# Modulation products of a two-layer hybrid block: column groups of the array and the shape of a loaded piece

## The chip, the core and the metric

One core of a Trainium2 chip. Metric: device time of one execution in microseconds (us). The kernel before takes 3295.98 us, the median of three runs (3289.71 to 3297.98). Engines are called as the profile calls them: PE (matmul), PEld (the weight load that goes with each matmul), DVE, ACT, POOL, and SP, whose queue SPq issues all DMAs here.

## The reference

Two layers (`DEPTH = 2`) over 1024 latent and 256 context tokens of 1024 features. Each layer begins with the modulation vectors, which the change is about; everything else uses them:

```
mod = silu(c) @ w_ada + b_ada            # w_ada: 1024 x 6144 per layer
sh1, sc1, g1, sh2, sc2, g2 = split(mod, 6)
cmod = silu(c_ctx) @ w_ada + b_ada       # the same weights for the context tokens
p = (x * (1 + sc1) + sh1) @ w_in         # then attention, convolution, mLSTM, w_out
x = layer_norm(ALPHA * x + g1 * y)
x = layer_norm(ALPHA * x + g2 * mlp(x * (1 + sc2) + sh2))
```

So per layer a vector of 1024 features is multiplied by a 1024 x 6144 matrix in float32, for two vectors (c and c_ctx). The matrix has 25 MB per layer and is read once.

## The kernel before, in words

The kernel is a program of one core in which a tile framework puts in the waits. Float32 accuracy of the large products comes from splitting both sides into a rounded part and a rest and summing three products in the PE's reduced float32 form. The modulation products are plain float32; the profile shows each of those matmuls as two records, that is two passes of the PE, each with a weight load.

**The modulation products (`ada_steps`, L160).** The 6144 columns of a layer are three rounds of 2048. A round has four 512-column chunks j = 0 to 3. The two vectors stand in `self.sil[:, k]`, 128 features by 32 columns (two used, the rest zero); they are the stationary side. The output of chunk j goes to the partitions 32j to 32j + 31 of one PSUM bank, so that it is made by the j-th group of 32 columns of the array. A round's sum runs over eight feature blocks k. The work is cut into closures, one for each loaded piece `wada`: a closure does the products of its piece and then issues the load of a later piece (`load(i + ahead)`, L187). A piece has n columns, n = 1024 / div:

- For the first layer, rounds 1 and 2 (L2027): div 1, pieces of 128 x 1024 (512 KB), four buffers, four loads ahead. The closures are taken by `tick(2)` in `p1_mlstm`, two after each token tile of the key and value projections (names `mk_ps`, `mv_ps`, lines L77 to L79). Round 0 of this layer has its own function, `ada_first`, which the change leaves alone.
- For the second layer, all three rounds: div 2, pieces of 128 x 512 (256 KB), two buffers, one load ahead. Round 0 (L2128) is done within the first layer's `mlp1`, one closure after every fourth step of its column loop (names `c_ps`, `cx_ps`). Rounds 1 and 2 (L2142) are done within the first layer's `mlp2`, one closure after every third product (names `o_ps`). All of these large products are issued at line L1365.

When a round's sum is complete, `fin` (L190) adds the bias on DVE, transposes four blocks on the PE (`adat`) and writes the vectors.

**What sets the order.** Each engine takes its instructions in the order in which the program was built, apart from a few that the framework moves. All loads and stores go through the one queue SPq in order; the load of a piece waits for the closure that last used its buffer. In `mlp2` the loads of hidden tiles (`hb`, L1643) and of weights (`rw`, L1347) stand in the same queue and wait for their own buffers.

**What mlp1 and mlp2 do.** Both are products in Winograd's form of 2 x 2 blocks. In `mlp2`, for every product of six (or three) matmuls of 512 columns, DVE or ACT adds or copies the result bank `o_ps` into `acc`, while DVE, ACT and POOL make the split operands `xs_hi`, `xs_lo` and `wm` of later products. In the second layer's `mlp2` there are no modulation products.

Of the kernel before, what the change touches and what calls it, by code (L numbers as in the profile page):

```python
# [14 lines left out]
PSUM = bass.MemoryType.PSUM  # L15
# [18 lines left out]
# columns of the regrouped input projection: a0 g0 | a1 g1 | mq | mk | mv mg | mo | cq ckv kr  # L34
COL_CONV, COL_MQ, COL_MK, COL_MV, COL_MO, COL_CQ = 0, 512, 768, 1024, 1296, 1552

# per-partition constants of a layer
# [8 lines left out]
class Kern:  # L46
# [11 lines left out]
    # ---------------------------------------------------------------- helpers  # L58
# [4 lines left out]
    def after(self, ins, prev):  # L63
        """issue ins behind prev (same engine)"""
        self.tc.add_manual_dep(ins.ins, prev.ins.name, mybir.DependencyInfo(
            mybir.DependencyClass.NoSync, mybir.DependencyReason.DATA), reason="pace")
        return ins

    def release_held(self, prev, n=1):
        """the n oldest sets of transposes kept back are issued behind prev"""  # L70
        for _ in range(min(n, len(self.held))):
            for ins in self.held.pop(0):
                self.after(ins, prev)
# [20 lines left out]
    def rsqrt_steps(self, pool, out, x, scale, eps, n):  # L94
        """out = 1 / sqrt(x * scale + eps) on [p, n], from an integer estimate and Newton steps; an instruction a step."""
# [15 lines left out]
    def rsqrt_act_steps(self, pool, out, x, scale, eps, n=1):  # L111
        """The same from ScalarE's square root and a Newton step."""
# [18 lines left out]
    # ---------------------------------------------------------------- set-up  # L131
# [28 lines left out]
    def ada_steps(self, l, rounds, raw_pool, ps, sm_pool, bufs, sm_tag="ada_bs", tag="wada", ahead=None, div=1):  # L160
        """Modulation vectors, four 512-column chunks a round: 0 sh1 sc1, 1 g1 sh2, 2 sc2 g2. A list of closures,
        each the products of one loaded piece and the load of a later one."""
# [6 lines left out]
        def load(i):  # L169
            if i < len(items):  # L170
                r, k, c0 = items[i]
                raw[i] = raw_pool.tile([P, n], F32, name="wada", tag=tag, bufs=bufs)
                nc.sync.dma_start(raw[i], a["w_ada"][l, r, k, :, c0:c0 + n])

        def step(i):
# [6 lines left out]
            w = raw.pop(i)  # L182
            for jj in range(n // 512):
                j = c0 // 512 + jj
                nc.tensor.matmul(acc[r][32 * j:32 * j + 32], self.sil[:, k], w[:, jj * 512:(jj + 1) * 512],  # L185
                                 start=(k == 0), stop=(k == KT - 1))
# [24 lines left out]
    def ada_first(self, raw_pool, ps, sm_pool, bufs):  # L211
        """sh1 and sc1 of the first layer by halves of the features. A closure a half."""
# [3 lines left out]
        def half(h):  # L216
# [4 lines left out]
            # even k in the rows 0:64, odd k in the rows 64:128  # L221
# [20 lines left out]
    # ---------------------------------------------------------------- split streams: hi / lo tiles [128, tile, k, 128 tokens]  # L242
# [14 lines left out]
    def make_u0(self, u, tmp, kk):  # L257
        """The modulated stream of the first layer, four feature blocks."""
# [9 lines left out]
    # ---------------------------------------------------------------- input projection  # L268
    def load_w(self, pool, src, c0, n, tag="w"):
        """columns c0:c0+n of a [128, 8, N] weight as split tiles of four k each."""  # L270
# [25 lines left out]
    # ---------------------------------------------------------------- phase 1: everything read from the modulated stream  # L296
    def p1_mlstm(self, l, u, last, ps, wp, hk, ml, steps, w=None):
        """mLSTM query (feature-major), key, value and gates (token-major)."""
# [12 lines left out]
        # the first layer's stream comes by halves of its features  # L311
# [36 lines left out]
    def residual_steps(self, l, pool):  # L348
        """Closures: alpha * (normalised stream * ln2_g + ln2_b) of the layer before, a token tile each, in place."""
# [16 lines left out]
    def residual_consts(self, l, pool, tag, bufs):  # L366
        """Constant part of the second residual, alpha * ln1_b + g2 * b_mlp2, of both kinds of tokens to DRAM."""
# [10 lines left out]
    def p1_conv(self, l, u, last, ps, wp, tmp):  # L378
        """Gated linear unit of the conv group (twice its value; the halves are in the taps)."""
# [17 lines left out]
    def p1_mla(self, l, u, last, ps, wp, wx, raw):  # L397
        """Compressed q / kv and the rotary key of a token tile, with the mean squares of their rms norms."""
# [25 lines left out]
    # ---------------------------------------------------------------- conv: depthwise taps, layer norm over channels, swish  # L424
    def conv_steps(self, l, last, ps, acc, tp, pool):
        """Closures in order: taps of channel half 0 on VectorE, half 1 on GpSimd, then the norm and swish."""
# [7 lines left out]
        def tap(t, dve, pool_):  # L434
            # behind the given instructions of the two engines
# [61 lines left out]
    def spill(self, pool, c, t0, src):  # L497
        """256 tokens of a row block of the concatenated heads, split and kept in DRAM until the output projection."""
# [6 lines left out]
    # ---------------------------------------------------------------- bidirectional mLSTM  # L505
    def mlstm_gates(self, ps, gp, sm):
        """Stabilised gate quantities. Row r = dir * 64 + tile * 4 + head, tokens along the free axis."""
# [70 lines left out]
        # decay of every chunk on the partitions of its head  # L578
# [15 lines left out]
    def mlstm(self, l, last, ps, ml, wk):  # L594
        nc = self.nc
        nto = NLT if last else NT
        # chunk states: every chunk's own update goes to its successor's slot, then the recurrence runs in place
# [72 lines left out]
    def mlstm_out(self, l, u, last, pm, wp, S, wk):  # L670
        """Output gate from its own projection, per-head normalisation of a pair of token tiles; its rows of the
        concatenated heads."""
# [18 lines left out]
        def pair(t0):  # L691
# [6 lines left out]
            # statistics of the eight (tile, head) rows; H holds twice the gated value  # L698
# [12 lines left out]
    # ---------------------------------------------------------------- latent attention  # L711
    def mla_norm(self, l, last, gi, tmp):
        """Normalised compressed q / kv of a group of tokens, in place."""
# [11 lines left out]
    def mla_rotate(self, tmp):  # L725
        """Rotary shared key, in place."""
# [13 lines left out]
    def mla_prep(self, l, last, ps, A, tmp, gi):  # L740
        """Compressed q / kv and the shared key of a group of tokens, feature-major, the former split."""
# [28 lines left out]
    def mla_values(self, l, ps, wq, A):  # L770
        """Values of all heads, token-major."""
# [20 lines left out]
    def attention(self, l, last, psc, ps, X, wq, A1, A, B, wqk0, taps, post):  # L792
        """Software pipeline over units of (head, 128 queries): scores of unit i are issued between the transposes of
        unit i - 2, the value products of an earlier group and the projections of a later one. The units of the
        context queries (256 of a head in one) lie between those of the last latent group of their head pair."""
        nc, a = self.nc, self.a
        sc = psc.tile([P, 2560], F32, name="sc")
        # buffers in the place of the stream: transposed exponentials; split keys and queries
# [116 lines left out]
        def transpose_parts(i, E, kts):  # L915
# [11 lines left out]
            while i0 < nk:  # L927
                # runs of consecutive key tiles, four to a bank
# [90 lines left out]
    # ---------------------------------------------------------------- rows, norms  # L1019
# [5 lines left out]
    def row_stats(self, pool, r, sm, tagp, junk, jb=2):  # L1025
        """(-mean, 1/std, -mean/std) of a token tile [128, 1024]; its row sums are in sm, else VectorE alone takes them."""
# [15 lines left out]
    def row_stats_steps(self, pool, st, r, sm, junk, jb, root=False):  # L1042
        """The same from row sums, the instructions behind the squares one by one."""
# [12 lines left out]
    def norm_rows(self, pool, r, sm, tagp, junk, jb=2):  # L1056
        """r = (r - mean) * rstd over the 1024 columns of a token tile."""
        st = self.row_stats(pool, r, sm, tagp, junk, jb)
        return self.nc.scalar.activation(r, r, AF.Identity, scale=st[:, 1:2], bias=st[:, 2:3])

    def next_stream(self, ps, x, t0, nt, rows, sc, sh, tmp, tag, hold=False):
        """rows: normalised token tiles t0..t0+nt; writes x = split(rows^T * sc + sh)."""
# [13 lines left out]
    def affine_cols(self, l, g0, b0, sc, sh, name):  # L1076
        """per-feature scale and shift of a modulated layer-normed stream: g*sc1, b*sc1 + sh  ([128, k, 2])"""
# [9 lines left out]
    # ---------------------------------------------------------------- output projection, first layer norm  # L1087
# [3 lines left out]
    def to_mats(self, ps, rows, sc, sh, pool, hold=False):  # L1091
        """rows: an even and an odd normalised token tile. For each kk the blocks B of rows^T * sc + sh (feature blocks
        kk, kk + 4 by the two tiles) and the sums T of them, split, in the order B11 T3 B21 B22 | T1 T2 T4. The four stages."""
# [35 lines left out]
    def xblock(self, xs, bx, c, s, kk, i):  # L1129
        """operand i of feature blocks kk, kk + 4 for the token pairs 2c, 2c + 1 (s: high or low part)"""  # L1130
# [8 lines left out]
    def xdst(self, xs, bx, pr):  # L1139
        """where to_mats puts its results for a pair of token tiles"""  # L1140
# [19 lines left out]
    def out_proj(self, l, last, p1, pw, ps, xs, W1, W2, R, R2):  # L1160
# [4 lines left out]
        def slot(s, t):  # L1165
            # the first four in the place of the first matrices, then a ring of three
# [9 lines left out]
        # weights, split, resident: the first three row blocks in W1; concatenated heads  # L1176
# [24 lines left out]
        def finish(t):  # L1201
            """residual, first norm, residual of the second norm"""
# [4 lines left out]
            while len(kept) > (t == 4 and not last) and t != 9:  # L1207
                # stores behind the loads that the next products wait for
# [32 lines left out]
            if t >= NLT:  # L1241
                # kept in memory until the space for its operands is free
# [10 lines left out]
        def gate(t, hf):  # L1253
            """the residual is in the row's place"""
# [14 lines left out]
        # the first tiles run side by side while weights arrive; the last ones are done early with the weights of W1  # L1269
# [37 lines left out]
        # the stages of the last two tiles' norms  # L1307
# [25 lines left out]
    def rslots(self, n):  # L1333
        """rows of two hidden tiles: three pairs of places in turn, those of the second product behind those of the first"""
# [19 lines left out]
    # ---------------------------------------------------------------- MLP, second layer norm  # L1354
# [917 lines left out]
```

## Time and profile before

| what | value |
|---|---|
| median of three runs | 3295.98 us (3289.71 to 3297.98) |
| profiled execution: span from first to last instruction | 3292.5 us |
| instructions | 49295 |
| DMA | 337.17 MB, mean 102 GB/s |

The page gives the span of the profiled execution; it does not tell a separate time with what lies around it. The span is 3.5 us under the median and within the three runs.

How to read the rows: a row of the timeline has its start, the time until its last instruction's end, engine, line, operation, names (out<-in), shape and count; equal instructions that follow each other are merged. Ends of matmuls are modelled, and rows overlap, so the pace of the PE is read from the starts of successive rows. A bracket tells idle time before a row and what ended it. `128*32 128x512` is an array of 128 rows by 32 columns with 512 columns streamed.

### The profile page before, as it was taken

What the parts mean: (1) busy time and instruction counts of PE and PEld (TensorE: products, weight loads), DVE (VectorE), ACT (ScalarE), POOL (GpSimd) and SP (SyncE); (2) the same over time, 40 slices, a digit from 0 to 9 for tenths busy, and PEclk for the clock granted to TensorE, in tenths of its full rate; (3) what the DMA queues carried; (4) which work ended last, traced back from release to release, by engine and by line L of the source; (5) the groups of instructions that cost most, each with busy time, mean ns of one, the idle gap of its engine ahead of it and who ended that gap; (6) DMA issues with size and microseconds to landing.
All of it is one profiled execution on the core that took longest, in us unless ns stands there. A gap on an engine that the chain in (4) does not pass through costs nothing.

```text
span 3292.5 us, 49295 instructions
## 1 busy us (share of the span) xinstructions
PE 3124.8 (95%) x18778; PEld 2540.8 (77%) x18778; DVE 2153.8 (65%) x3914; ACT 1356.8 (41%) x2572; POOL 1322.3 (40%) x1138
## 2 busy tenths in 40 slices
PE   7999999999899999999998999999999899999986
PEld 4778877777789999766677777877767799977775
DVE  3275688755854433767779445588757855578997
ACT  2122566672433333432332621466663433343332
POOL 0021488320221111466665251266411422258885
PEclk9999999999899999999999998999999899999998
DMA  8521100026433233444334332100025333333322
GB/s 263 187 68 40 49 18 17 14 83 225 159 120 101 97 99 103 157 126 144 114 109 134 142 111 50 56 21 14 14 92 213 109 109 108 106 128 97 102 94 105
DMA packets 179021, 337.17 MB, mean 102 GB/s; under 512 B 14016, under 2 KB 85696, under 8 KB 178784
## 3 DMA queue, kind: packets, MB, share of 16 engines
q1 hardware_dynamic: 178784, 334.03, 31.6%
q8 instruction: 147, 2.41, 0.3%
q14 instruction: 90, 0.74, 0.1%
HBM read 253.05 MB, written 80.92 MB: 101 GB/s over the span
## 4 chain that ended last, share of the span: by engine, by line
PE 71%; DVE 14%; issue 5%; POOL 3%; ACT 3%; DMA 3%; SPq 0%; DVEq 0%; POOLq 0%; ACTq 0%
PE c_ps L1365 18%; PE o_ps L1365 13%; PE pv L861 4%; PE et_ps L936 4%; PE ada L185 3%; PE cx_ps L1365 3%; DVE acc L2168 2%; PE sc L77 2%; PE sc L78 2%; PE sc L79 2%; PE o_ps L658 1%; PE y_ps L79 1%; DMA W<-md 1%; POOL h_s L2168 1%; PE y_ps L77 1%
## 5 line engine op out<-in xcount | busy, mean ns | idle before, releaser
L1365 PE MATMUL c_ps<-xs_hi,wm 128*128 128x256 f32 x2560 | 511.1, 288 | 11.5 <-DVE rw L2168 8.1
L1365 PEld LDWEIGHTS c_ps<-xs_hi,wm 128*128 128x128 f32 x2560 | 422.1, 195 | 38.7 <-DVE hb L1427 11.7
L1365 PE MATMUL o_ps<-xs_hi,xs_lo 128*128 128x512 f32 x1458 | 380.1, 398 | 27.8 <-DVE acc L2168 20.7
L1365 PE MATMUL c_ps<-xs_lo,wm 128*128 128x256 f32 x1280 | 366.6, 286 | 3.2 <-DVE xs_lo L2168 3.2
L1365 PEld LDWEIGHTS o_ps<-xs_hi,xs_lo 128*128 128x128 f32 x1458 | 271.9, 190 | 120.8 <-DVE acc L2168 34.6
L2168 DVE TENSOR_TENSOR acc<-o_ps,acc 128x512 f32<-128x512 f32 x405 | 271.8, 683 | 101.7 <-PE o_ps L1365 99.4
L1365 PEld LDWEIGHTS c_ps<-xs_lo,wm 128*128 128x128 f32 x1280 | 249.6, 195 | 3.9 <-DVE xs_lo L2168 3.6
L84 ACT COPY et<-et_ps 128x512 f32<-128x512 f32 (+1 forms) x392 | 198.4, 515 | 97.7 <-PE et_ps L936 93.1
L1365 PE MATMUL c_ps<-bx,wm 128*128 128x256 f32 x1536 | 229.2, 288 | 4.5 <-ACT bx L2168 3.0
L92 DVE TENSOR_TENSOR wm<-rw,wm 128x512 fp32r<-128x512 f32 x175 | 140.2, 803 | 111.2 <-ACT wm L84 110.4
L1365 PE MATMUL o_ps<-wm,xs_lo 128*128 128x512 f32 x783 | 208.0, 397 | 4.4 <-DVE acc L2168 3.5
L1365 PEld LDWEIGHTS c_ps<-bx,wm 128*128 128x128 f32 x1536 | 205.2, 195 | 7.9 <-ACT bx L2168 3.5
L84 ACT CAST wm<-rw 128x512 fp32r<-128x512 f32 x175 | 108.4, 620 | 231.2 <-PE c_ps L1365 177.8
L1395 POOL TENSOR_TENSOR w_s<-w_s,rw 128x512 f32<-128x512 f32 x30 | 40.0, 1332 | 397.3 <-DVE wm L92 397.3
L861 PE MATMUL pv<-et,V 128*64 128x256 f32 x1312 | 193.3, 391 | 0.0
L1365 PEld LDWEIGHTS o_ps<-wm,xs_lo 128*128 128x128 f32 x783 | 147.5, 191 | 50.8 <-DVE acc L2168 8.6
L77 PE MATMUL sc<-kq 128*128 128x512 f32 (+1 forms) x400 | 165.9, 415 | 8.4 <-DVE E L908 7.4
L1429 ACT ACTIVATE hb<-c_ps,fm 128x256 f32<-128x256 f32 x240 | 112.8, 474 | 144.3 <-PE c_ps L1365 137.6
L2168 POOL TENSOR_TENSOR xs_hi<-rw,xs_hi 128x512 fp32r<-128x512 f32 x94 | 138.4, 1487 | 78.9 <-ACT xs_hi L2168 78.8
L449 POOL TENSOR_TENSOR conv_acc<-conv_acc,tap 128x656 f32<-128x656 f32 x120 | 154.5, 1287 | 8.8
L908 DVE TENSOR_SCALAR_CACHE_REDUCE E<-sc 128x1280 f32<-128x1280 f32 x91 | 135.2, 1486 | 26.7 <-PE sc L79 25.9
L909 ACT ACTIVATE E<-E,nm 128x1280 f32<-128x1280 f32 x91 | 124.4, 1368 | 66.4 <-DVE E L908 66.1
(506 smaller groups left out, 7968.6 us busy)
## 6 DMA issues: line engine op xcount, KB each, us to landing
rw<-in_w_mlp SPq DMA_DIRECT2D x126, 512.0 KB
hb<-h_d SPq DMA_DIRECT2D x72, 512.0 KB
h_d<-hb SPq DMA_DIRECT2D x64, 512.0 KB
wada<-in_w_ada SPq DMA_DIRECT2D x48, 512.0 KB
wada<-in_w_ada SPq DMA_DIRECT2D x96, 256.0 KB
cat_d<-sp SPq DMA_DIRECT2D x144, 128.0 KB
w_raw<-in_w_in SPq DMA_DIRECT2D x20, 512.0 KB
xs_hi<-cat_d SPq DMA_DIRECT2D x18, 512.0 KB
```

Source lines behind the costliest of these rows:

```text
L77: mm(ps, lh, rh, start=first, stop=False)
L79: return mm(ps, ll, rh, start=False, stop=last)
L84: return nc.scalar.copy(out, in_)
L92: return h, e.tensor_tensor(lo, src, hi.bitcast(F32), ALU.subtract)
L449: nc.gpsimd.tensor_tensor(aj[:, c], aj[:, c], m, ALU.add)
L861: nc.tensor.matmul(pvs[G][64 * e:64 * e + 64, 0], self.V[:, kt, h * 64:h * 64 + 64], ets[G, e][:, kt], start=(i == 0), stop=(i == nk - 1))
L908: dve = nc.vector.tensor_scalar(E, s[:, c], -1.0, None, ALU.mult, ALU.min, accum_out=nm[:, 0:1])
L909: act = nc.scalar.activation(E, E, AF.Exp, bias=nm[:, 0:1], scale=-1.0, accum_out=nm[:, 1:2])
L936: nc.tensor.transpose(pt[:, j], E[:, (i0 + j) * P:(i0 + j + 1) * P], self.ident)
L1365: ins = self.nc.tensor.matmul(ps, x, y, start=first and i == 0, stop=i == len(todo) - 1, skip_group_check=True)
L1429: self.nc.scalar.activation(h[:, :, q], b, AF.Identity, bias=f[:, FM_B1 + 2 * i + q % 2:FM_B1 + 2 * i + q % 2 + 1])
L2168: ins = f(*a, **k)
```

## The change

A piece no longer holds n neighbouring columns of one or two chunks; it holds n/4 columns, the same ones, of each of the four chunks. The closure then makes four products, one for each 32-column group of the array, of 256 columns (first layer) or 128 columns (second layer). The bytes loaded, the number of loads, the closures and their places stay.

```diff
@@ -170,7 +171,8 @@
                 raw[i] = raw_pool.tile([P, n], F32, name="wada", tag=tag, bufs=bufs)
-                nc.sync.dma_start(raw[i], a["w_ada"][l, r, k, :, c0:c0 + n])
+                nc.sync.dma_start(raw[i].rearrange("p (j c) -> p j c", j=4),
+                                  a["w_ada"][l, r, k].rearrange("p (j c) -> p j c", j=4)[:, :, c0 // 4:(c0 + n) // 4])
@@ -179,11 +181,10 @@
-            w = raw.pop(i)
-            for jj in range(n // 512):
-                j = c0 // 512 + jj
-                nc.tensor.matmul(acc[r][32 * j:32 * j + 32], self.sil[:, k], w[:, jj * 512:(jj + 1) * 512],
-                                 start=(k == 0), stop=(k == KT - 1))
+            w = raw.pop(i).rearrange("p (j c) -> p j c", j=4)
+            for j in range(4):
+                nc.tensor.matmul(acc[r][32 * j:32 * j + 32, c0 // 4:(c0 + n) // 4], self.sil[:, k], w[:, j],
+                                 start=(k == 0 and c0 == 0), stop=(k == KT - 1 and c0 + n == 2048), skip_group_check=True)
```

A contiguous run of the load shrinks from 4 KB to 1 KB in the first layer, and from 2 KB to 512 bytes in the second. The program has 512 modulation matmuls in place of 160, on the lines L185 (before) and L186 (changed).

On the PE, in `mlp2` of the first layer (`o_ps`: result bank of a large product; `ada`: the modulation sum), there stood before:

```order
L185 MATMUL ada_12669<-wada,sil 32x512
L1365 MATMUL o_ps<-xs_hi,xs_lo 128x512 x6
L1365 MATMUL o_ps<-wm,xs_lo 128x512 x6
L1365 MATMUL o_ps<-xs_hi,xs_lo 128x512 x6
L185 MATMUL ada_12669<-wada,sil 32x512
```

and now:

```order
L186 MATMUL ada_12829<-wada,sil 32x128 x4
L1366 MATMUL o_ps<-xs_hi,xs_lo 128x512 x6
L1366 MATMUL o_ps<-wm,xs_lo 128x512 x6
L1366 MATMUL o_ps<-xs_hi,xs_lo 128x512 x6
L186 MATMUL ada_12829<-wada,sil 32x128 x4
```

The places are the same; one matmul of 512 columns has become four of 128.

On the PE, in the key projection of the first layer (`mk_ps`), before:

```order
L77 MATMUL mk_ps<-w_hi,x_hi 128x256
L185 MATMUL ada_560<-wada,sil 32x512 x4
L77 MATMUL mk_ps<-w_hi,x_hi 128x256
```

and now:

```order
L77 MATMUL mk_ps<-w_hi,x_hi 128x256
L186 MATMUL ada_560<-wada,sil 32x256 x8
L77 MATMUL mk_ps<-w_hi,x_hi 128x256
```

Two closures stand together here, so that four matmuls on the four column groups have become eight. Apart from the modulation rows, the PE's order differs in ten single places by one or two matmuls, that of SPq by two moved DMAs, and those of DVE, ACT and POOL not at all.

## Rows read from the trace of the kernel before

**Rows 1.** The page: span, busy times, the chain that ended last by engine and line.
```profile
span 3292.5 us, 49295 instructions
PE 3124.8 (95%) x18778; PEld 2540.8 (77%) x18778; DVE 2153.8 (65%) x3914; ACT 1356.8 (41%) x2572; POOL 1322.3 (40%) x1138
PE 71%; DVE 14%; issue 5%; POOL 3%; ACT 3%; DMA 3%; SPq 0%; DVEq 0%; POOLq 0%; ACTq 0%
PE c_ps L1365 18%; PE o_ps L1365 13%; PE pv L861 4%; PE et_ps L936 4%; PE ada L185 3%; PE cx_ps L1365 3%; DVE acc L2168 2%; PE sc L77 2%; PE sc L78 2%; PE sc L79 2%; PE o_ps L658 1%; PE y_ps L79 1%; DMA W<-md 1%; POOL h_s L2168 1%; PE y_ps L77 1%
```

**Rows 2.** Stretches: busy us and count of PE, PEld, DVE, ACT, POOL; clock, DMA, GB/s.
```profile
57.00:135.00 78.00, 78.00 (x579) 61.01 (x581) 16.13 (x38) 17.57 (x35) 0.00 (x0) 1.00 0.82 258
135.00:200.00 65.00, 60.11 (x388) 45.67 (x380) 44.69 (x118) 20.02 (x43) 19.97 (x19) 1.00 0.24 59
919.00:1340.00 421.00, 419.24 (x3262) 389.28 (x3261) 175.57 (x258) 140.68 (x274) 81.34 (x64) 1.00 0.33 108
1350.00:1692.00 342.00, 340.06 (x1282) 221.04 (x1281) 242.18 (x338) 118.32 (x214) 211.65 (x191) 1.00 0.43 133
2960.00:3160.00 200.00, 189.59 (x821) 152.77 (x820) 181.97 (x250) 74.92 (x141) 176.11 (x146) 1.00 0.33 106
```

**Rows 3.** Waits (total us, times, longest): PE from 1340, DVE from 1360, PE from 2960.
```profile
PE o_ps L1365 <- ACT xs_lo L2168: 1.9, 1, 1.9
...
DVE acc L2168 <- PE o_ps L1365: 90.4, 97, 3.2
...
PE o_ps L1365 <- DVE acc L2168: 10.4, 12, 1.2
```

**Rows 4.** Timeline of the PE in the first layer's mlp2, two closures.
```profile
1397.00 1.05 PE L185 MATMUL ada<-wada,sil 128*32 128x512 f32 x2
1397.98 1.66 PE L1365 MATMUL o_ps<-xs_hi,xs_lo 128*128 128x512 f32 x6
1399.47 1.53 PE L1365 MATMUL o_ps<-wm,xs_lo 128*128 128x512 f32 x6
1400.84 1.52 PE L1365 MATMUL o_ps<-xs_hi,xs_lo 128*128 128x512 f32 x6
1402.29 1.05 PE L185 MATMUL ada<-wada,sil 128*32 128x512 f32 x2
...
1397.45 0.59 PE L185 MATMUL ada<-wada,sil 128*32 128x512 f32 x1
```

**Rows 5.** Timeline of PE and PEld, first layer's key projection, two closures together.
```profile
76.77 1.06 PE L185 MATMUL ada<-wada,sil 128*32 128x512 f32 x8
77.76 0.39 PE L77 MATMUL mk_ps<-w_hi,x_hi 128*128 128x256 f32 x1
...
76.76 0.16 PEld L185 LDWEIGHTS ada<-wada,sil 128*32 128x32 f32 x8
```

**Rows 6.** Timeline of the PE: ten float32 passes of 128 columns, starts 180.44 to 181.44.
```profile
180.44 1.28 PE L639 MATMUL st_ps<-mqT,kT 64*128 64x128 f32 x10
```

**Rows 7.** Timeline of the PE in the first layer's mlp1: one closure, a pair, the first two.
```profile
947.70 1.04 PE L185 MATMUL ada<-wada,sil 128*32 128x512 f32 x2
948.67 0.38 PE L1365 MATMUL c_ps<-xs_hi,wm 128*128 128x256 f32 x1
...
1331.82 1.05 PE L185 MATMUL ada<-wada,sil 128*32 128x512 f32 x4
1332.80 0.38 PE L1365 MATMUL c_ps<-xs_hi,wm 128*128 128x256 f32 x1
...
923.47 1.71 PE L185 MATMUL ada<-wada,sil 128*32 128x512 f32 x4 [1.62 <-DMA wada<-in_w_ada]
...
925.80 1.60 PE L1365 MATMUL cx_ps<-xc,wm 128*128 128x256 f32 x12
927.24 1.58 PE L1365 MATMUL cx_ps<-xc,w_a 128*128 128x256 f32 x12
```

**Rows 8.** The stretches of rows 2 for the instructions of `ada` alone (PE, PEld, DVE).
```profile
919.00:1340.00 421.00, 32.04 (x64) 4.26 (x64) 0.29 (x1) 1.00 0.33 108
1350.00:1692.00 342.00, 66.91 (x128) 8.79 (x128) 0.68 (x1) 1.00 0.43 133
```

**Rows 9.** Timelines of SPq and PE: loads of pieces, and closures that use them.
```profile
919.04 0.94 SPq L173 DMA_DIRECT2D wada<-in_w_ada  x2
...
1403.37 0.33 SPq L173 DMA_DIRECT2D wada<-in_w_ada  x1
1412.86 1.05 PE L185 MATMUL ada<-wada,sil 128*32 128x512 f32 x2
...
1480.36 0.38 SPq L173 DMA_DIRECT2D wada<-in_w_ada  x1
1486.87 1.05 PE L185 MATMUL ada<-wada,sil 128*32 128x512 f32 x2
...
86.35 0.37 SPq L173 DMA_DIRECT2D wada<-in_w_ada  x1
92.87 0.64 PE L185 MATMUL ada<-wada,sil 128*32 128x512 f32 x4
```

## The prediction

> **What bounds the kernel now.** I read the page first [rows 1]: the PE is busy 95% of the span and holds 71% of the chain that ended last, and the modulation products alone (`ada`, L185) are 3% of that chain, about 99 us. So time taken from them counts, if the PE is the limit where they stand. The stretches [rows 2] say that it is: the PE is busy 78.0 of 78 us in the first layer's projections, 419 of 421 us in mlp1 and 340 of 342 us in mlp2 (clock 1.00 in all three), while DVE is at 21%, 42% and 71%. The waits [rows 3] agree: from 1340 to 1700 the PE waits once, 1.9 us, and DVE waits 90.4 us for the PE.
>
> Then the timeline. In mlp2 a lone closure's two passes start at 1397.00 and 1397.45, and the next large product at 1397.98 [rows 4]: 0.98 us for one matmul of 512 columns on one column group, the other three groups idle. Its closures stand 5.29 us apart with no gap, 18 large matmuls between them. In the key projection two closures stand together, four matmuls on the four groups, and the next matmul starts 0.99 us after the first [rows 5]. So the groups already run side by side there: four products cost what one costs, and three more groups add 0.01 us. All eight weight loads are issued within 0.16 us. This row is what the forecast stands on.
>
> **The change, part by part.**
>
> *A lone closure in mlp2 and mlp1.* It held one matmul of 512 columns; it will hold four of 128, two passes each: sixteen instructions (a weight load and a matmul per pass), as many as the packed closures of [rows 5] hold now. The price of a pass: 512 columns take 0.45 us from one pass's start to the next [rows 4]; float32 passes of 128 columns elsewhere start 1.00 / 9 = 0.11 us apart [rows 6], a quarter. From the first start to the next work there are now 0.45 + 0.53 us. Taking two passes of 512 columns at 4 x 0.107 = 0.43 (the 0.11 of [rows 6] less a small fixed part), some 0.12 us are left, which I keep: 0.03 between the passes, 0.09 behind the second. New: 0.11 + 0.03 + 0.11 + 0.09 + 0.02 for the stagger of three more groups = 0.36 us. Saved: 0.98 - 0.36 = **0.62 us** per closure. Bounds: if only the passes count, 0.22 us, saved 0.76; if the sixteen instructions go at the pace of weight load and matmul in mlp1, 1.44 / 12 = 0.12 us per pair [rows 7], 8 x 0.12 = 0.96 us, saved nothing. I take 0.62 because [rows 5] show sixteen instructions of exactly this kind without such a pace: their eight weight loads are out in 0.16 us, not 0.96.
>
> There are 96 closures for the second layer: 128 / 2 in mlp2, all alone, and 64 / 2 in mlp1 [rows 8], of which 28 stand alone (0.97 us each, [rows 7]) and two pairs remain. So 92 x 0.62 = **57.0 us**.
>
> *The two pairs in mlp1.* At 1331.82 two closures on two groups take 0.98 us now [rows 7]. After, both use all four groups, so the second queues behind the first: 0.36 + 2 x 0.13 = 0.62, saved 0.36. The first pair, at 923.47, waits for its loads, issued at 919.04 [rows 7, 9]; only what follows the second landing shrinks: 0.4 to 0.6, I take 0.5. Together 0.9 us.
>
> *The first layer.* Sixteen pairs of closures. Each group had two passes of 512 columns, it will have four of 256: two more switches between passes, 2 x 0.03 = 0.05 us. 16 x 0.05 = 0.8 us lost. Nothing is won, since all four groups were busy already.
>
> *The loads.* Their number, bytes and places stay; each has four times as many runs. In the first layer the DMA engines are 0.82 busy at 258 GB/s, that is 258 / (0.82 x 16) = 19.7 GB/s per busy engine; the lowest rate in a neighbouring stretch is 59 / (0.24 x 16) = 15.4 GB/s [rows 2]. If all 32 pieces (16.8 MB) fell to that rate, the engines would be busy 16.8 / 16 / 15.4 against 16.8 / 16 / 19.7, 68 against 53 us: 15 us more in a stretch that has 0.18 x 78 = 14 us free. A piece is issued 6.5 us before its use there (86.35 to 92.87, [rows 9]). So the cost lies between nothing and some 8 us; I take 1 us, since the pieces have the run length (1 KB) of the projection weights that go through the same stretch. In mlp2 a load is issued two closures ahead, 9.5 us (1403.37 to 1412.86), and the slowest pair I see, at 919.04, came 4.4 us after its issue and with its wait told [rows 9, 7]. With closures 4.67 us apart 8.5 us remain: nothing lost, and it would take a doubling to lose anything.
>
> *What is late next.* DVE has 90.4 us of waits for the PE in the mlp2 stretch [rows 3]; 64 x 0.62 = 40 us of those go, so it stays behind the PE in the mean, at 242 / 302 = 80% busy; POOL at 212 / 302 = 70%. Two places give something back. The closures at the very start of mlp2 stand ahead of the one PE wait there (1.9 us, ended by ACT's operand): two of them lose their gain, 1.2 us. And some loads are issued late because SPq stands behind loads whose buffers DVE and POOL free: 1480.36 is used at 1486.87, 6.5 us later instead of 9.5 [rows 9]. If those issues do not move up with the PE, a closure finds its piece late by up to 2 us; I count 3 us in all.
>
> **The sum.** 57.0 + 0.9 - 0.8 - 1.0 - 1.2 - 3.0 = 51.9, about 52 us. The profiled span is 3292.5 us [rows 1]; 3240.5 after. The median of the runs is 3.5 us over that span, so the time becomes **3244 us**.
>
> **The rivals.**
>
> *A: helpers limit mlp2.* The second layer's mlp2 has the same loop without modulation products. There DVE is at 91% and POOL at 88%, and the PE idles 10.4 of 200 us waiting for DVE's sums [rows 2, 3]. If the first layer's mlp2 behaves so once its closures are short, 5% of 302 us, 15 us, come back: gain 37 us, **3259 us**. Against: DVE would be at 80%, not 91%.
>
> *B: the groups do not fill.* The change would not do what it says if short passes were limited by how fast the PE is fed: at 0.12 us per weight load and matmul [rows 7] a closure takes 0.96 us as now: gain 0, and the first layer's are longer anyway (passes of 0.24), so **3297 us**. For: a closure's work per instruction falls to a quarter. Against: [rows 5]. [...]
>
> *C: slower, weight loads that wait for running matmuls.* All four groups use all 128 rows. If a weight load could not pass a matmul on the same rows, the eight passes of a closure would go one by one: 8 x 0.13 + 0.09 = 1.13 us against 0.98, 96 x 0.15 = 14 us lost; in the first layer sixteen passes of 0.24 and 0.1 make 3.9 us against 0.99, 16 x 2.9 = 47 us lost: **3357 us**. It decides as soon as the groups overlap by less than one part in seven in the second layer. Against: [rows 5], where such a rule would give 8 x 0.45 = 3.6 us and the trace has 0.99. [...]
>
> **How the numbers follow.** A measurement of this kernel can tell about 0.3%, 10 us, from no change. My forecast has 0.80, A 0.11, B 0.05, C 0.04. Faster by over 0.3% holds the forecast and A: 0.91; within 0.3%: B, 0.05; slower: C, 0.04. The range: upward, nothing given back is 58 us (3238), and 0.66 instead of 0.62 per closure another 4 us (3234); the bound of 0.76 I hold for out of reach; downward it takes in A, and with it the 8 us of the first layer's loads against the forecast: **3234 to 3262 us**.
>
> **What would show it.** In the profile after: closures of the second layer as eight matmul records with starts a few ns apart in two bunches, and the next large product 0.3 to 0.45 us after the first (right), or near 1 us (B, C); closures in mlp2 4.7 us apart; the first layer's groups at 1.05 us; `ada` down from 3% to about 1.5% of the chain; PE waits in mlp2 under 5 us (A: about 15); no new wait of the PE for `wada` before 135 us. The forecast is wrong if the PE's busy time per closure falls and the span doesn't: then the 52 us went into waits for DVE, POOL or the loads, and the waits of the PE between 1350 and 1650 name it.

## The result and the profile after

| kernel | time, us | ratio to before |
|---|---|---|
| before, run beside it | 3296.98 (3289.71 to 3298.78) | |
| changed | 3249.48 (3240.57 to 3256.05) | 0.986 (0.984 to 0.988) |

The change makes the kernel 47.5 us faster; 3244 us was forecast, in a range from 3234 to 3262. The profiled execution of the changed kernel has a span of 3254.3 us against 3292.5 [rows 1].

The page of the changed kernel: span, busy times, the chain that ended last by engine and by line, DMA.

```profile
span 3254.3 us, 50699 instructions
PE 3087.3 (95%) x19482; PEld 2558.5 (79%) x19482; DVE 2156.0 (66%) x3914; ACT 1355.4 (42%) x2572; POOL 1330.1 (41%) x1138
PE 70%; DVE 14%; issue 5%; POOL 4%; DMA 4%; ACT 3%; SPq 0%; DVEq 0%; POOLq 0%; ACTq 0%
PE c_ps L1366 18%; PE o_ps L1366 12%; PE pv L862 4%; PE et_ps L937 4%; PE cx_ps L1366 3%; DVE acc L2169 2%; PE sc L77 2%; PE sc L78 2%; PE sc L79 2%; PE ada L186 1%; PE o_ps L659 1%; DMA W<-md 1%; POOL h_s L2169 1%; DVE rw L2169 1%; PE y_ps L79 1%
DMA packets 228179, 337.27 MB, mean 104 GB/s; under 512 B 14016, under 2 KB 151232, under 8 KB 227936
```

`ada` has gone from 3% to 1% of the chain [rows 1], and the PE still holds 70% of it. The bytes are those of before (337.17 MB) but for 0.1 MB, in 228179 packets in place of 179021.

The timeline of PE and PEld of the changed kernel: two closures in mlp2, then the two pairs of closures in mlp1, then the first layer.

```profile
1393.35 0.43 PE L186 MATMUL ada<-wada,sil 128*32 128x128 f32 x8
1393.70 1.66 PE L1366 MATMUL o_ps<-wm,xs_lo 128*128 128x512 f32 x6
1395.20 1.53 PE L1366 MATMUL o_ps<-xs_hi,xs_lo 128*128 128x512 f32 x6
1396.56 1.52 PE L1366 MATMUL o_ps<-wm,xs_lo 128*128 128x512 f32 x6
1398.01 0.43 PE L186 MATMUL ada<-wada,sil 128*32 128x128 f32 x8
...
1398.01 0.16 PEld L186 LDWEIGHTS ada<-wada,sil 128*32 128x32 f32 x8 [0.35 <-issue]
...
936.55 0.43 PE L186 MATMUL ada<-wada,sil 128*32 128x128 f32 x8 [0.43 <-DMA wada<-in_w_ada]
...
939.23 0.43 PE L186 MATMUL ada<-wada,sil 128*32 128x128 f32 x8 [1.58 <-DMA wada<-in_w_ada]
...
1329.28 0.65 PE L186 MATMUL ada<-wada,sil 128*32 128x128 f32 x16
1329.85 0.39 PE L1366 MATMUL c_ps<-xs_hi,wm 128*128 128x256 f32 x1
...
72.54 1.07 PE L186 MATMUL ada<-wada,sil 128*32 128x256 f32 x16
73.54 0.39 PE L77 MATMUL mk_ps<-w_hi,x_hi 128*128 128x256 f32 x1
...
85.89 0.64 PE L186 MATMUL ada<-wada,sil 128*32 128x256 f32 x8
87.14 0.64 PE L186 MATMUL ada<-wada,sil 128*32 128x256 f32 x8 [0.60 <-DMA wada<-in_w_ada]
87.71 0.38 PE L77 MATMUL mk_ps<-w_hi,x_hi 128*128 128x256 f32 x1
```

A closure of the second layer has eight passes now, and the next large product starts 0.35 to 0.36 us after the first of them (1393.35 to 1393.70, 1398.01 to 1398.37), where [rows 4] had 0.98. The eight weight loads are out in 0.16 us, as in [rows 5]. The closures of mlp2 stand 4.66 us apart; before 5.29. The pair of mlp1 takes 0.57 us (1329.28 to 1329.85), before 0.98 [rows 7]. A pair of the first layer takes 1.00 us (72.54 to 73.54), before 0.99 [rows 5]. One of them, at 85.89, found its second piece late.

Waits of the changed kernel (total us, times, longest): the PE from 57 to 1700, the PE from 1340 to 1700, and DVE from 1360 to 1700.

```profile
PE ada L186 <- DMA wada<-in_w_ada: 3.9, 6, 1.6
...
PE o_ps L1366 <- ACT xs_lo L2169: 2.2, 1, 2.2
PE ada L186 <- DMA wada<-in_w_ada: 1.3, 3, 0.7
PE o_ps L1366 <- DVE acc L2169: 1.1, 1, 1.1
...
DVE acc L2169 <- PE o_ps L1366: 56.7, 80, 2.6
```

Up to the last modulation product the PE waits 2.2 + 1.3 = 3.5 us here, before 1.9 [rows 3]. The 1.1 us for DVE come behind it, at 1687 us; the kernel before has the same wait at 1729 us, outside the window of [rows 3]. DVE's waits for the PE fell from 90.4 us and did not run out. The 56.7 us hold some of what follows, since this kernel is some 42 us ahead by then; from 1357 to 1648 us, the same work as in [rows 3], they are 52.3.

Stretches of the changed kernel: busy us and count of PE, PEld, DVE, ACT, POOL; clock, DMA, GB/s.

```profile
57.00:135.00 78.00, 77.39 (x687) 63.97 (x687) 17.02 (x39) 17.60 (x35) 0.00 (x0) 1.00 0.82 255
136.00:310.00 174.00, 164.15 (x887) 128.57 (x886) 99.33 (x234) 33.66 (x60) 33.94 (x26) 0.85 0.20 48
919.00:1340.00 421.00, 417.88 (x3564) 405.68 (x3565) 188.55 (x281) 150.93 (x294) 86.66 (x67) 1.00 0.34 114
1350.00:1640.00 290.00, 286.49 (x1593) 211.48 (x1592) 232.57 (x325) 111.76 (x203) 206.58 (x179) 1.00 0.49 153
```

DVE is busy 232.6 of 290 us in mlp2, 80%, and POOL 71%. The stretch from 136 to 310 us, the mLSTM, contains no closure after 137 us; its granted clock is 0.85. In the kernel before it was 0.96:

```profile
136.00:310.00 174.00, 163.52 (x999) 132.93 (x999) 111.91 (x268) 38.72 (x69) 37.38 (x30) 0.96 0.22 57
```

What the PE did ahead of that hardly differs: from 136 to 165 us it is busy 27.8 of 29 us (before 27.5), with a clock of 1.00 in both, and from 165 to 190 us 21.6 of 25 (before 21.7). There the clock falls to 0.95, and to 0.84 from 190 to 215 us; before it is 1.00 in both. The PE's waits from 136 to 310 us are nearly those of before (the longest, for DVE's `num`, 4.5 us against 4.8), while the same matmuls take longer. These are the rows of one group in the kernel before and in the changed one (busy us, mean ns, idle time before it):

```profile
L658 PE MATMUL o_ps<-v,W 128*128 128x65 f32 x160 | 28.1, 301 | 0.1
...
L659 PE MATMUL o_ps<-v,W 128*128 128x65 f32 x160 | 32.0, 333 | 0.0
```

**Where the time went.** For each PE instruction that both kernels have, other than those of `ada`, I took its start in the changed kernel less its start before; the table gives the change of that difference over each stretch (times of the kernel before). Minus is earlier. The kernel `change_3` is the change once more, in another execution; `again`, a third, is told of below.

| stretch, us | what is there | change, us | again, us | change_3, us |
|---|---|---|---|---|
| 60 to 134 | first layer's pairs | +0.8 | 0.0 | +0.2 |
| 170 to 310 | mLSTM, no closure | +16.2 | -4.2 | -3.3 |
| 904 to 1330 | mlp1, up to its last pair | -16.6 | -18.2 | -17.6 |
| 1330 to 1690 | that pair and mlp2 | -39.4 | -39.9 | -39.3 |
| 0 to 3270 | all | -38.3 | -63.2 | -61.8 |

The closures of the second layer give 56.0, 58.0 and 56.9 us in three executions. What differs between the executions lies where there are no closures, above all in the mLSTM.

### The profile page after: what moved, and what is told of

It is laid out like the page before. It is cut to its first block, busy times and chain, and to the rows that moved or that the text cites. A ratio compares the mean times of both kernels' runs of the same rounds, so it can differ in the third digit from the quotient of the medians.

```text
span 3254.3 us, 50699 instructions
## 1 busy us (share of the span) xinstructions
PE 3087.3 (95%) x19482; PEld 2558.5 (79%) x19482; DVE 2156.0 (66%) x3914; ACT 1355.4 (42%) x2572; POOL 1330.1 (41%) x1138
## 2 busy tenths in 40 slices
DMA packets 228179, 337.27 MB, mean 104 GB/s; under 512 B 14016, under 2 KB 151232, under 8 KB 227936
## 4 chain that ended last, share of the span: by engine, by line
PE 70%; DVE 14%; issue 5%; POOL 4%; DMA 4%; ACT 3%; SPq 0%; DVEq 0%; POOLq 0%; ACTq 0%
PE c_ps L1366 18%; PE o_ps L1366 12%; PE pv L862 4%; PE et_ps L937 4%; PE cx_ps L1366 3%; DVE acc L2169 2%; PE sc L77 2%; PE sc L78 2%; PE sc L79 2%; PE ada L186 1%; PE o_ps L659 1%; DMA W<-md 1%; POOL h_s L2169 1%; DVE rw L2169 1%; PE y_ps L79 1%
```

## The experiments

**1. The second layer's part alone** (`l1_only`). Loads and products are those of the change for div 2 and those of before for div 1.

```diff
+                if div > 1:
                     nc.sync.dma_start(raw[i].rearrange("p (j c) -> p j c", j=4), ...)
+                else:
+                    nc.sync.dma_start(raw[i], a["w_ada"][l, r, k, :, c0:c0 + n])
```

Expected:

> The change in the second layer's closures alone; the first layer's pieces and products stay as before. Theory 1 (the gain is per closure of the second layer, 0.62 us each; what the profiled run of the change lost, 16 us between 180 and 290, is a lower granted clock in the mLSTM and no cost of the new products): everything up to 900 us runs as in the kernel before, clock there included; from mlp1 on 56 us are gained, closures 0.36 us to the next product, 13.5 us apart in mlp1 and 4.67 in mlp2. Time 3297 - 56 = 3241 us, ratio 0.983. Theory 2 (the new short products cost clock or DMA wherever they stand): less than 50 us gained, with a granted clock under 1.00 in mlp1 or mlp2, or waits of the PE for pieces of over 3 us in all.

Measured: 3237.95 us (3223.97 to 3242.44), ratio 0.982 (0.979 to 0.984). From 904 to 1690 us its instructions gain 56.0 us. So the whole gain is the second layer's. One part of theory 1 missed: the stretch ahead of 900 us did not run as before. This profile too loses 9.3 us between 170 and 310 us, at a clock of 0.89, though nothing ahead of 904 us differs from the kernel before:

```profile
136.00:310.00 174.00, 164.90 (x940) 131.81 (x939) 104.56 (x241) 37.26 (x66) 34.94 (x27) 0.89 0.23 55
```

The profile of experiment 6, whose first layer is also that of before, loses 12.6 us there, at 0.87. So a loss of this kind does not need the change.

**2. The first layer's part alone** (`l0_only`): the same switch the other way round (`if div == 1:`).

Expected:

> The change in the first layer's closures alone. Theory 1: pairs of closures take 1.00 instead of 0.99 us, one or two pieces come late by up to 1 us, so the projections end about 2 us later; and the mLSTM behind them may or may not get a lower clock, as in executions of any form: 3297 to 3300 us where it does not, up to 3313 where it does, and both in one set of executions. Theory 2 (the first layer's new form costs some 10 us by itself, by its loads or by the clock): 3307 us or more in every execution, ratio 1.003 to 1.005, with the clock from 165 to 330 us always lower than before.

Measured: 3289.86 us (3275.36 to 3304.84), ratio 0.999 (0.997 to 1.001). Between 60 and 134 us nothing is lost (0.0 us). Its timeline of the PE:

```profile
85.54 1.07 PE L189 MATMUL ada<-wada,sil 128*32 128x256 f32 x16
86.54 0.39 PE L77 MATMUL mk_ps<-w_hi,x_hi 128*128 128x256 f32 x1
```

A pair takes 1.00 us, and the pair that stood late in the first profile of the change finds its pieces here. So sixteen passes of 256 columns cost what eight of 512 cost with all four groups in use (0.99 us, [rows 5]), and the late load at 85.89 was one execution's.

**3. Short products on one column group** (`one_group`). The pieces and loads are those of before; for div 2 the one matmul of 512 columns is cut into four of 128, all on the same group.

```diff
-                nc.tensor.matmul(acc[r][32 * j:32 * j + 32], self.sil[:, k], w[:, jj * 512:(jj + 1) * 512],
-                                 start=(k == 0), stop=(k == KT - 1))
+                m = 128 if div > 1 else 512
+                for cc in range(0, 512, m):
+                    nc.tensor.matmul(acc[r][32 * j:32 * j + 32, cc:cc + m], self.sil[:, k], w[:, jj * 512 + cc:jj * 512 + cc + m],
+                                     start=(k == 0 and cc == 0), stop=(k == KT - 1 and cc + m == 512), skip_group_check=True)
```

Expected:

> The kernel before, but each second-layer closure makes its 512 columns of one chunk in four products of 128 columns, all on one column group: as many instructions as the change, the loads of before. If the gain comes from the groups running side by side: eight passes one behind another, 7 x 0.13 + 0.11 + 0.1 = 1.1 to 1.2 us from the first start to the next product against 0.98, 96 x 0.2 = 19 us lost, 3310 to 3316 us. If short products were quicker by themselves: as the change, about 3245. If the feed of instructions were the limit, the closure would take the same 0.36 us as in the change or longer than 1.2 us.

Measured: 3293.0 us (3287.2 to 3300.29), ratio 0.999 (0.998 to 1.001). Timeline of PE and PEld in mlp2, and the line's weight loads there (ns: shortest, median, longest):

```profile
1396.06 1.06 PE L187 MATMUL ada<-wada,sil 128*32 128x128 f32 x8
1397.05 1.65 PE L1367 MATMUL o_ps<-wm,xs_lo 128*128 128x512 f32 x6
...
1396.06 0.79 PEld L187 LDWEIGHTS ada<-wada,sil 128*32 128x32 f32 x8 [0.35 <-issue]
...
L187 PEld LDWEIGHTS ada<-wada,sil x504: 105/110/111, 1350.1 to 1683.0; 128*32 128x32 f32 x168
```

Eight short passes on one group take 0.99 us to the next product; two long ones took 0.98 [rows 4]. The direction is what the theory of groups side by side said (no gain from short products), the size is not: it put a pass and its weight load at 0.13 us and expected a loss. The loads add nothing to the passes: eight of 0.11 us each, one behind the other, fill 0.79 of the same 0.99 us, though all of them are for one column group and its 128 rows (`128*32`). So cutting a product costs nothing, and only the four groups bring the 0.62 us.

**4. The change once more** (`again`).

Expected:

> The change once more, to see how its executions spread. Theory 1: times between 3238 and 3258 us that follow the core's mean granted clock (0.971 to 0.977), at about 13 us per 0.004 of clock; in an execution with 0.975 or more the stretch from 180 to 290 us is at most 5 us longer than in the kernel before. Theory 2: all executions near 3255 us.

Measured: 3239.25 us (3231.15 to 3246.37), ratio 0.984 (0.981 to 0.986), profiled span 3229.4 us. It has the -58.0 us of the closures (table above) and none of the +16 us of the mLSTM, as theory 1 said for a clock of 0.975 or more. Theory 2 fell. The numbers of theory 1 fit less well: two of the five executions lie under its range, and from 3246.37 us at 0.973 to 3231.15 at 0.979 the time falls by 10 us per 0.004, not 13.

**5. Old products, two column groups at a time** (`pair_old`). Everything is as before, but in mlp2 one place takes two pieces, that is two neighbouring groups.

```diff
+        def two(i):
+            step(i, False)
+            step(i + 1, False)
+            load(i + 2)
+            load(i + 3)
...
-            steps = () if last else self.ada_steps(l + 1, (1, 2), R2, aux, R2, 2, "g", "g", 1, 2)
+            steps = () if last else self.ada_steps(l + 1, (1, 2), R2, aux, R2, 2, "g", "g", 2, 2, True)
```

Expected:

> The products and pieces of the kernel before (one matmul of 512 columns on one column group for each piece). Only in the first layer's mlp2 two pieces, for neighbouring column groups, are taken by one closure, so that two groups can work side by side; there are 32 such places in place of 64. Theory 1 (what counts is that the groups work side by side; the length of a product does not matter by itself): a pair takes the 0.98 us that one closure took, 32 x 0.98 = 31 us go, all of it between 1345 and 1690 us of the span: ratio to before about 0.990. Theory 2 (the gain of the change came from short products or from shorter runs of a load): pairs of 512 columns take 1.8 to 2.0 us, ratio 1.00. If loads become late, since they are issued a pair ahead, the PE's waits on wada in mlp2 show it; I expect under 5 us of them.

Measured: 3259.28 us (3246.95 to 3263.22), ratio 0.990 (0.987 to 0.992); from 1330 to 1690 us 34.7 us are gained. Its timeline of the PE in mlp2:

```profile
1395.66 1.05 PE L185 MATMUL ada<-wada,sil 128*32 128x512 f32 x4
1396.65 1.66 PE L1374 MATMUL o_ps<-wm,xs_lo 128*128 128x512 f32 x6
...
1405.04 1.05 PE L185 MATMUL ada<-wada,sil 128*32 128x512 f32 x4
```

Two products of 512 columns on two groups take 0.99 us, what one takes alone (0.98, [rows 4]). No product is shorter and no load has shorter runs here, and more than half of the change's gain is there: the groups side by side are its cause. The gain is 3 us over the expected 31. A place among the large products has a price beyond the stretch from its first start to the next product: in [rows 4] the six large matmuls behind a closure take 1.49 us from start to start, the next six 1.37, and the last six ahead of the next closure 1.45. That is 0.12 + 0.08 = 0.2 us on the way in and out, and taking two places together saves it once more: pairs stand 9.38 us apart (1395.66 to 1405.04), two closures of before 2 x 5.29 = 10.58, so a pair saves 1.20 us. Here 30 places hold two closures and four hold one; of 30 x 1.20 = 36.0 us, 34.7 came, and the PE waits some 1 us longer than before in the stretch.

**6. The change's products, two closures at a time** (`pair_l1`): experiment 1 with `two(i)` in mlp2.

Expected:

> The change for the second layer's pieces alone, and in mlp2 two closures taken together, so that eight products follow each other: two for each group. Theory 1 (a closure costs its passes and a fixed way in and out; a pair pays the way once): the next large product starts 0.57 us after the first start, as behind the one pair in mlp1 of the change, in place of 2 x 0.36 = 0.72: 32 x 0.15 = 5 us less than the change for the second layer alone, ratio to before 0.980 (that run had 0.982, 0.979 to 0.984, so the medians may not tell the two apart, and the timeline must). Rival (late loads: pieces are issued a pair ahead and are needed two at a time): waits on wada in mlp2 rise from 4 us to over 9 us and take the gain back: ratio 0.982 to 0.985.

Measured: 3228.51 us (3219.53 to 3233.12), ratio 0.981 (0.978 to 0.983). Its timeline of the PE:

```profile
1402.04 0.64 PE L189 MATMUL ada<-wada,sil 128*32 128x128 f32 x16
1402.61 1.67 PE L1384 MATMUL o_ps<-xs_hi,xs_lo 128*128 128x512 f32 x6
...
1404.82 4.25 PE L1384 MATMUL o_ps<-xs_hi,xs_lo 128*128 128x512 f32 x18
1408.91 0.84 PE L1384 MATMUL o_ps<-wm,xs_lo 128*128 128x512 f32 x3
...
1411.04 0.64 PE L189 MATMUL ada<-wada,sil 128*32 128x128 f32 x16
```

The pair takes 0.57 us, as expected. Its distance to the next is 9.00 us, with 36 large matmuls of (1408.91 - 1404.82) / 18 = 0.227 us in it; two closures of the change fill 2 x 4.66 = 9.32. So a pair saves 0.32 us, twice what was expected: the 0.15 of the expectation and some 0.2 for the way in and out. Against experiment 1 the stretch from 1330 to 1690 us is 11.6 us shorter (-49.5 against -37.9). The rival's late loads did not come: the profile has no wait of the PE for `wada` from 1340 us on.

**7 and 8. The change and the change with pairs on one chip** (`change_3`, `pair_all`). The second is the changed kernel with `two(i)` in mlp2.

Expected of the first:

> The change itself, run on the same chip as the next kernel, to compare the two. Ratio to before 0.983 to 0.987, 3238 to 3250 us. Theory 1 (the products of each closure fix the gain, and the rest of the spread is the clock that was granted between 136 and 310 us): closures 13.50 us apart in mlp1 and 4.67 in mlp2 again, and the span over or under 3240 us goes with the granted clock of 136 to 310 us (0.85 with 3254 us and 0.98 with 3229 us so far).

Expected of the second:

> The change with two closures taken together in the first layer's mlp2. The timelines of the runs so far give the price of a lone closure in mlp2 as its distance to the next less 18 large matmuls of 0.227 us: 5.29 - 4.08 = 1.21 us before and 4.67 - 4.08 = 0.59 after, and of a pair 9.00 - 36 x 0.227 = 0.84. So a pair saves 2 x 0.59 - 0.84 = 0.34 us, 32 x 0.34 = 11 us of mlp2. Theory 1: 10 to 12 us less than the change run beside it, ratio to before 0.979 to 0.983. Rival (what the pair gains is lost to DVE, which is then 84% busy in that stretch): waits of the PE for acc in mlp2 over 5 us, and the same time as the change.

Measured: 3238.78 us (3232.49 to 3243.05), ratio 0.983 (0.981 to 0.985), and 3221.24 us (3212.53 to 3232.03), ratio 0.978 (0.975 to 0.980). From 1330 to 1690 us the pairs bring 9.9 us (-49.2 against -39.3), just under the 10 to 12 that were expected. The medians differ by 17.5 us; the other 7.6 us are not in that stretch, and nothing in the change to pairs accounts for them. With executions of `pair_all` up to 20 us apart (3212.53 to 3232.03), they are not shown to belong to the pairs. The rival is not there. DVE is busy 232.48 of 282 us from 1350 to 1632, 82% (84% was expected), and from 1340 to 1700 us the PE waits for it three times, but as often in the change (first row, `again`) as with pairs (second row), and behind the last modulation product (third and fourth row, `pair_all`):

```profile
PE o_ps L1366 <- DVE acc L2169: 4.0, 3, 1.7
...
PE o_ps L1375 <- DVE acc L2178: 4.4, 3, 1.7
...
1616.16 0.64 PE L186 MATMUL ada<-wada,sil 128*32 128x128 f32 x16
...
1656.93 1.67 PE L1375 MATMUL o_ps<-xs_lo 128*128 128x512 f32 x6 [1.15 <-DVE acc L2178]
```

The first of the two has its mLSTM stretch at a clock of 0.98 and a span of 3230.7 us:

```profile
136.00:310.00 174.00, 164.10 (x1028) 133.75 (x1028) 113.08 (x272) 39.20 (x71) 39.18 (x31) 0.98 0.22 57
```

`pair_all` is faster than both kernels: 78 us under before and 17.5 us under the change.

## Why the prediction was right, point by point

- **The closure.** Forecast 0.36 us in place of 0.98, measured 0.35 to 0.36; forecast 0.62 us saved, and the distance fell from 5.29 to 4.66. The step it stood on, [rows 5], was the right one: experiments 3 and 5 show that it is the groups and not the length of the products. One thing the price left out is the wider spacing of the large matmuls around a closure (experiment 5); it is there before and after the change, so the difference of 0.62 held.
- **The two pairs in mlp1.** The last one takes 0.57 us, forecast 0.62. At the start of mlp1 the two closures of the first pair stand apart in the changed kernel (936.55 and 939.23), and each waits for its load, 0.43 and 1.58 us; the forecast had one wait for the pair. mlp1 gave 16.6 to 18.2 us against 28 x 0.62 + 0.5 = 17.9.
- **The first layer's products and loads.** Forecast +1.8 us, measured 0.0 to +0.8. Both halves were too high. The extra switches cost next to nothing (a pair takes 1.00 us, 0.99 before), and the DMA rate held: 255 GB/s at 0.82 busy, against 258 at 0.82 [rows 2]. One late load, 0.6 us of waiting, in one of the three profiles of the change.
- **Late loads and the start of mlp2.** This is the term that was mis-sized. Forecast 3.0 + 1.2 us given back; from 1330 to 1690 us there is room for 64 x 0.62 + 0.4 = 40.1 us, and 39.3 to 39.9 came, so 0.2 to 0.8 us were given back. From 1340 us on the PE's waits for `wada` are 1.3, 0.5 and 1.0 us in the three profiles, where 3 were counted. The wait for ACT, at which 1.2 us were to be lost, grew only from 1.9 us to 2.2, 2.4 and 2.3.
- **The sum.** For the second layer's closures 57.0 + 0.9 - 1.2 - 3.0 = 53.7 us were forecast, and 56.0 to 58.0 measured. The forecast span was 3240.5; two profiles of the change have 3229.4 and 3230.7, the first one 3254.3. In those two, 5 to 6 us come from terms of the sum that were too cautious, and 3 to 4 from the mLSTM, at a clock of 0.98 against 0.96 before. The sum has no term for that clock. That the measured time, 3249.5, is only 5.5 us above the forecast is in part luck: the gain was forecast too small, and the clock took back more than that. The first profile loses 16 us by it (0.85 against 0.96); the other three executions behind the median were not profiled, so for them it is not shown, though their mean granted clocks of 0.971 to 0.976 fit. Against the kernel before run beside it, the change gained 47.5, 54.8 and 60.4 us in its three sets of runs; 52 was forecast.
- **Rival A (helpers limit mlp2)** did not come: DVE is at the 80% that the forecast worked out, and over the same work its waits for the PE fell by 38.1 us (90.4 to 52.3), forecast 40. Up to the last modulation product the PE does not wait for DVE's sums in any of the three profiles of the change, nor with pairs.
- **Rival B (feeding)** fell: eight passes with their weight loads need 0.36 us, not 0.96, and the eight weight loads are out within 0.16 us.
- **Rival C (weight loads that wait)** fell twice: in the change, where a closure takes 0.36 us and not 1.13, and in experiment 3, where all passes and loads are for the same rows and the same column group. There eight loads of 0.11 us and eight passes together take 0.99 us to the next product, not 8 x (0.11 + 0.11) = 1.8, an estimate from the loads of experiment 3 and the 0.11 us of a pass in [rows 6]. How a load and a running pass share the rows, no run here shows.

**What stays open.** Over the 44 executions of the kernel before with a mean granted clock of 0.973 to 0.982, the time follows the mean granted clock closely: 3278.5 us at 0.982, 3308.9 us at 0.973, on a straight line 2.85 us for each 0.001. The executions of the change have 0.971 to 0.980 (one record of 0.93 aside). Why one execution of a program is granted less in the mLSTM than another was not tried. Whether the change lowers the clock a little on average can't be told from 13 executions: against the kernel before run beside it the mean is 0.976 to 0.977 in `again` (without that record) and 0.976 to 0.976 in `change_3`, and among the variants 0.977 to 0.977 in `l1_only`, 0.979 to 0.976 in `pair_all` and 0.975 to 0.978 in `pair_l1`.

## What to carry to other kernels

A matmul with 32 stationary columns takes one of four column groups here (`128*32` in [rows 4]), and four products on the four groups cost what one of the same length costs (0.99 us against 0.98). So give the four groups different output columns of the same product in one go. Look for the place where the kernel does this already and read the price there. Where such small products stand between large ones, the way in and out is paid at each place (0.2 us here), so fewer places with more products each were a second, separate gain (9.9 us in `pair_all` against the change, 11.6 in `pair_l1` against `l1_only`).

## What was not expected of the hardware

- Eight float32 passes of 128 columns on one column group cost the same as two of 512, 0.99 against 0.98 us: their eight weight loads of 0.11 us, all for that one group, add nothing to it.
- A closure costs some 0.2 us more than the stretch from its first start to the next product: the six large matmuls just ahead of it take 1.45 us from start to start and the six just behind it 1.49, the six between 1.37 [rows 4].
- The strided load takes SPq longer to issue. These are the rows of the loads (ns: shortest, median, longest) before and after, 328 against 546 ns for each of 128 loads. SPq has 0% of the chain in both kernels, and what late loads cost in mlp2 is 0.5 to 1.3 us in all.

```profile
L173 SPq DMA_DIRECT2D wada<-in_w_ada x128: 327/328/837, 57.9 to 1678.7; - x128
```

```profile
L174 SPq DMA_DIRECT2D wada<-in_w_ada x128: 539/546/1461, 59.0 to 1638.1; - x128
```
